# Up-projection of the last 1224 tokens by seven products of halves, in two rounds

## The chip, the cores and the metric

The kernel runs on one core of a Trainium2 chip. The metric is the time of one execution on the device in microseconds (us). The engines are named as in the profile: PE (TensorE, matmuls), PEld (its weight loads), DVE (VectorE), ACT (ScalarE), POOL (GpSimd) and SP (SyncE, which issues the DMAs).

## The reference

One step of a one-layer decoder over 2048 prompt tokens and 8 sample tokens (2056 columns here), width 1024, all in float32. What matters for the change, with h the tokens after attention, pooling and the output projection:

```python
def _mlp(h, g, w_up, w_down):                 # w_up 1024 x 4096, w_down 4096 x 1024
    a = jax.nn.relu(rmsnorm(h, g) @ w_up)
    return (a * a) @ w_down
def _ple(h, p, g, w_gate, w_ple):             # w_gate 1024 x 1024
    gate = jax.nn.sigmoid(rmsnorm(h, g) @ w_gate)
    return (p @ w_ple) * gate
hp = hp + _mixer_out(outs, lses, pooled, w_out[i])
hp = hp + _mlp(hp, norm_mlp_g[i], w_up[i], w_down[i])
hp = hp + _ple(hp, p_prompt[i], ple_norm_g[i], w_ple_gate[i], w_ple[i])
y_prompt = rmsnorm(hp, final_norm_g)
```

The sample tokens go the same way.

## The kernel before, in words

Activations lie transposed: features on the 128 partitions, tokens along the columns. Each float32 operand is split into a high part rounded to fp32r and a low part (the rest), and a product of two operands is three matmuls (high by high, high by low, low by high), so one group over 1024 features is 8 x 3 = 24 matmuls into one PSUM bank (`group`, line 341). `load_w` (line 327) fetches a weight tile by DMA, makes its high part on POOL or ACT and its low part on DVE.

The tokens are taken in two parts: X, the first 832 columns (`CX`, two chunks of 416), and Y, the last 1224 (`CY`, chunks of 416, 416 and 392). After attention the order is: output projection of X, MLP of X, output projection of Y (with the norm of X's gate beside it), gate of X (with the norm of Y's MLP beside it), MLP of Y (lines 1652 to 1670; the final norm and output of X beside its first half), gate of Y's first two chunks, and `last_gate` for the third chunk, with the output of the first two beside it.

`mlp` (line 1319) goes through 4096 hidden features in 8 blocks of 512 for Y. In a block it computes, for each of 4 tiles of 128 hidden features and each chunk, one group of 24 matmuls, then relu, square, the high part (ACT, lines 1344 to 1347) and the low part (DVE); then, for each of 8 output tiles and each chunk, a group of 12 matmuls, which DVE adds to the accumulator held in SBUF (line 1356 on). Weights go through four raw buffers and a ring of two finished tiles.

`Stat` (line 1177) sums squares per token; its `finish` lets PE sum over partitions, DVE and ACT take 1/rms (`newton`), and PE turn the result into a row on all partitions (line 1204). `gate` (line 1397) per output tile: 24 matmuls a chunk, sigmoid (ACT, line 1410), times the embedding part (POOL), added to the accumulator (DVE), square (line 1419), and scaling by the final norm's weight in place (line 1425).

SBUF is cut by hand: `Arena.alloc` gives column ranges of a few large tiles (`mem_f` float32, `mem_r` fp32r, and pieces `ma`, `mb` that change hands between them). A range that is given again waits, instruction by instruction, for the last use of the same columns. Background work (`bg`) is a Python generator that `Pace` advances as groups are written down. The framework orders each engine's instructions ahead of time, by its own cost model, earlier-written work first among what is ready; on the chip each engine runs its list in order.

## Time and profile before

| what | value |
|---|---|
| time, median of 3 runs | 2725.55 us (2722.32 to 2728.67) |
| profiled execution, its own time | 2727.2 us |
| its span, first to last instruction | 2725.4 us |
| instructions | 42893 |
| busy, DVE | 1510.3 us (55%) |
| busy, ACT | 1078.2 us (40%) |
| HBM read / written | 209.47 / 60.30 MB |

Busy time is the time in which an engine has at least one instruction running. Matmuls overlap each other, so the time from one matmul to the next is read from a stretch's length and the count of matmuls in it, not from the duration of one. The span is what the trace covers; the execution's own time is 1.8 us more. In the trace, output projection of Y lies at about 1500 to 1640 us, gate of X to 1735, MLP of Y to 2600, gate of Y to 2717.

### The profile page before, as it was taken

How to read it: one execution, taken by the hardware profiler on the slowest of the kernel's cores; microseconds unless marked ns; L12 is line 12 of the kernel's file. 1: busy time of each engine (PE TensorE's matmuls, PEld its weight loads, DVE VectorE, ACT ScalarE, POOL GpSimd, SP SyncE). 2: the span in 40 equal slices, each digit the busy share in tenths (PEclk: the TensorE clock that was granted, in tenths of full speed). 3: DMA queues.
4: the chain of work that ended last, by engine and by line, in shares of the span. 5: the costliest groups of instructions: out<-in, count | busy, mean ns of one | idle time of the engine just before them, and what ended most of it. 6: DMA issues, size and time to landing. Idle time of an engine off the chain costs nothing.

```text
span 2725.4 us, 42893 instructions
## 1 busy us (share of the span) xinstructions
PE 2645.6 (97%) x15686; PEld 2526.9 (93%) x15686; DVE 1510.3 (55%) x3373; ACT 1078.2 (40%) x2021; POOL 674.8 (25%) x938
## 2 busy tenths in 40 slices
PE   8999899998999999999999899999999999999998
PEld 6888899977988999999999898999999999999998
DVE  6747866665586666665764747432232322322675
ACT  6221354553354355354455424423223123132354
POOL 2414745433253121021222616100000000000163
PEclk9999999999999999999999999999999999999999
DMA  7464344476153333342322545331111111111134
GB/s 249 132 180 121 87 125 125 115 210 191 55 153 107 84 85 86 97 108 71 95 77 66 167 139 152 127 105 39 43 42 40 39 39 39 39 39 39 53 85 150
DMA packets 385936, 272.50 MB, mean 100 GB/s; under 512 B 91466, under 2 KB 349205, under 8 KB 385717
## 3 DMA queue, kind: packets, MB, share of 16 engines
q1 hardware_dynamic: 385653, 269.74, 34.5%
q8 instruction: 123, 2.02, 0.3%
q14 instruction: 88, 0.72, 0.1%
q10 hardware_dynamic: 72, 0.02, 0.0%
HBM read 209.47 MB, written 60.30 MB: 99 GB/s over the span
## 4 chain that ended last, share of the span: by engine, by line
PE 65%; DVE 4%; DMA 4%; POOL 3%; ACT 2%; issue 2%; SPq 0%; DVEq 0%; POOLq 0%; ACTq 0%
PE bank L190 65%; DVE mem_r L196 2%; DVE mem_f L196 1%; POOL mem_ma L196 1%; DMA mem_f<-in_cache_attn_kv_dram 1%; POOL mem_f L196 1%; PE bank L1466 0%; POOL mem_r L199 0%; DMA mem_ma<-poo_s 0%; SPq L187 0%; DVE mem_r L1229 0%; DMA mem_ma<-h_s 0%; DMA mem_f<-poo_s 0%; DVE mem_ma L196 0%; ACT mem_r L931 0%
## 5 line engine op out<-in xcount | busy, mean ns | idle before, releaser
L190 PE MATMUL bank<-mem_r 128*128 128x416 f32 (+10 forms) x13608 | 2447.2, 338 | 42.7 <-DVE mem_f L196 8.1
L190 PEld LDWEIGHTS bank<-mem_r 128*128 128x128 f32 (+2 forms) x13608 | 2305.2, 184 | 118.3 <-DVE mem_f L196 11.9
L196 DVE TENSOR_TENSOR mem_r<-mem_f,mem_r 128x512 fp32r<-128x512 f32 (+3 forms) x568 | 418.2, 742 | 198.9 <-ACT mem_r L335 117.8
L196 DVE TENSOR_TENSOR mem_f<-bank,mem_f 128x416 f32<-128x416 f32 (+3 forms) x488 | 273.4, 567 | 241.4 <-PE bank L190 231.2
L335 ACT CAST mem_r<-mem_f 128x512 fp32r<-128x512 f32 x256 | 157.0, 620 | 575.0 <-PE bank L190 560.5
L196 DVE TENSOR_TENSOR mem_r<-mem_mb,mem_r 128x416 fp32r<-128x416 f32 (+6 forms) x236 | 152.8, 656 | 341.3 <-ACT mem_r L1347 304.1
L199 POOL TENSOR_SCALAR mem_r<-mem_f 128x512 fp32r<-128x512 f32 (+1 forms) x188 | 143.3, 769 | 260.3 <-PE bank L190 177.9
L196 POOL TENSOR_TENSOR mem_ma<-mem_mb,mem_f 128x416 f32<-128x416 f32 x1 | 1.4, 1431 | 828.5 <-ACT mem_f L1205 828.5
L776 DVE CUSTOM_DVE_ANT_0 bank<-bank,mask 128x256 f32<-128x256 f32 (+3 forms) x504 | 159.7, 339 | 40.8 <-PE bank L190 36.6
L1344 ACT ACTIVATE mem_mb<-bank 128x392 f32<-128x392 f32 (+1 forms) x160 | 81.8, 511 | 253.0 <-PE bank L190 253.0
L199 POOL TENSOR_SCALAR mem_r<-mem_r 128x256 fp32r<-128x256 f32 (+1 forms) x117 | 84.1, 731 | 206.3 <-PE bank L190 174.2
L859 POOL TENSOR_SCALAR_AFFINE_SELECT mem_ma<-mem_ma 128x256 f32<-128x256 f32 (+2 forms) x148 | 75.7, 531 | 173.0 <-ACT mem_ma L868 99.2
L196 DVE TENSOR_TENSOR mem_ma<-bank,mem_ma 128x416 f32<-128x416 f32 (+2 forms) x104 | 63.4, 610 | 86.3 <-PE bank L190 76.9
L190 PE MATMUL bank<-mem_mb,mem_r 128*64 128x64 f32 (+4 forms) x494 | 100.6, 323 | 5.7 <-DVE mem_r L196 2.1
L190 PEld LDWEIGHTS bank<-mem_mb,mem_r 128*128 128x128 f32 (+1 forms) x494 | 79.7, 177 | 14.9 <-DVE mem_r L196 2.7
L196 POOL TENSOR_TENSOR mem_f<-mem_f 128x416 f32<-128x416 f32 (+2 forms) x52 | 68.8, 1326 | 96.9 <-DMA mem_f<-in_cache_attn_kv_dram 31.4
L196 DVE TENSOR_TENSOR mem_r<-mem_ma,mem_r 128x512 fp32r<-128x512 f32 (+4 forms) x88 | 63.1, 719 | 39.1 <-ACT mem_r L880 28.3
L859 POOL TENSOR_SCALAR_AFFINE_SELECT mem_mb<-mem_mb 128x256 f32<-128x256 f32 (+2 forms) x76 | 33.7, 463 | 185.1 <-ACT mem_mb L868 126.4
L1345 ACT ACTIVATE mem_mb<-mem_mb 128x416 f32<-128x416 f32 (+1 forms) x128 | 70.0, 547 | 3.8
L199 POOL TENSOR_SCALAR mem_r<-mem_mb 128x512 fp32r<-128x512 f32 (+3 forms) x61 | 51.5, 852 | 77.2 <-PE bank L190 52.4
L1347 ACT CAST mem_r<-mem_mb 128x416 fp32r<-128x416 f32 (+1 forms) x128 | 68.5, 535 | 3.7
L776 DVE DVE_READ_ACCUMULATOR2_ANT mem_ma<- 128x1 f32 (+1 forms) x512 | 68.8, 134 | 0.0
(256 smaller groups left out, 1893.9 us busy)
## 6 DMA issues: line engine op xcount, KB each, us to landing
mem_f<-in_w_up_dram SPq DMA_DIRECT2D x128, 256.0 KB
mem_f<-in_w_down_dram SPq DMA_DIRECT2D x128, 256.0 KB
mem_f<-in_w_in_dram SPq DMA_DIRECT2D x64, 256.0 KB
out_dram<-mem_f SPq DMA_DIRECT2D x55, 256.0 KB
mem_f<-in_cache_attn_kv_dram SPq DMA_DIRECT2D x48, 256.0 KB
mem_f<-in_w_ple_gate_dram SPq DMA_DIRECT2D x48, 256.0 KB
mem_f<-in_x_prompt_dram SPq DMA_DIRECT2D x64, 128.0 KB
xT_s<-mem_f SPq DMA_DIRECT2D x32, 256.0 KB
```

The lines of the kernel that those rows point to most:

```text
L190: PE.matmul(out, l, r, start=start, stop=stop)
L196: eng.tensor_tensor(out, a, b, op=op)
L199: G.tensor_scalar(out, src, 1.0, 1.0, op0=ALU.mult, op1=ALU.mult)
L335: hi(w[:, 0, k0 : k0 + kk], raw)
L776: V.tensor_tensor_reduce(src, src, mask, 1.0, -3e38, ALU.add, ALU.max, mcol[: src.shape[0], col : col + 1])
L859: G.affine_select(out=p, in_=p, pattern=[[0, nblk], [sign, w]], compare_op=ALU.is_ge, fill=0.0, base=base, channel_multiplier=-sign)
L1344: S.activation(a, ps[:, :ln], AF.Relu)
L1345: S.activation(sq, a, AF.Square)
L1347: S.copy(x[:, 0], sq)
```

## The change

Y is cut into four chunks of 306 columns (`HY`). The MLP of Y runs in two rounds (`mlp_seven`), one for each pair of chunks (c0, c1). In a round the up-projection is taken as a product of 2 x 2 blocks: features halved (tile k with tile k + 4), hidden features halved (c with c + 2048), columns halved (c0 with c1). Instead of eight block products there are seven, on sums and differences of the blocks (`w_sums`, `z_sums`, made before the split into high and low parts), each 12 matmuls of 306 columns. PSUM banks 0, 1 and 3 collect them:

```diff
+    SEVEN = ((0, 0, 0, 1), (3, 3, 2, 5), (5, 5, 0, 6), (1, 1, 1, 2), (4, 4, 0, 7), (6, 2, 2, 3), (2, 6, 0, 4))
+    OPENS = (1, 2, 5)
...
+            for slot_w, slot_z, b, p in SEVEN:
+                n, last = 0, 3 * len(x) - 1
+                for k, xk in enumerate(x):
+                    for i, q in PASSES:
+
+                        PE.matmul(bu[b][:, :ln], ws[k // 2].at(slot_w, i, k % 2), xk[:, q, slot_z],
+                                  start=n == 0 and p in OPENS, stop=n == last, skip_group_check=p not in OPENS)
+                        n += 1
+                fill.work(12 * ln)
+                ps = bu[b][:, :ln]
+                if p in (1, 5, 6, 4):
+                    S.copy(z[:, {1: 0, 5: 2, 6: 3, 4: 1}[p]], ps)
+                else:
+                    i = {2: 0, 3: 3, 7: 2}[p]
+                    tt(V, z[:, i], ps, z[:, i], ALU.add)
+                if p == 3:
+                    fill.late()
+            S.activation(z, z, AF.Relu)
+            S.activation(z, z, AF.Square)
+            r = rl[blk, j] = z_parts_view(rls(), 4)
+            S.copy(r[:, 0], z)
+            tt(V, r[:, 1], z, f(r[:, 0]), ALU.subtract)
```

In each tuple stand the weight's slot, the activation's slot, the bank and a number; a product whose number is not in `OPENS` adds to what its bank holds already, after that has been copied out. An up section is seven products and yields 4 x 306 columns of hidden values; a down section is 8 groups of 12 matmuls. `sections` orders them: up 0 (two sections), then up and down sections by turns, up 7 (two sections), then the last four down sections. There are 16 of each in a round.

```diff
+    def w_sums(raw, s):
+        tt(V, s[:, 0], raw[:, 0], raw[:, 3], ALU.subtract)
+        tt(V, raw[:, 3], raw[:, 3], raw[:, 2], ALU.add)
+        tt(V, s[:, 1], raw[:, 3], raw[:, 0], ALU.subtract)
+        tt(V, s[:, 2], raw[:, 1], s[:, 1], ALU.subtract)
...
+        def early(self):
+            w_sums(self.a, self.b)
+            self.p4 = self.parts(self.a, self.w4, 4)
+
+        def late(self):
+            self.p3 = self.parts(self.b, self.w3, 3)
+
+        def parts(self, src, ring, n):
+            w = [x.rearrange("p (s n) -> p s n", s=n) for x in ring()]
+            S.copy(w[0], src)
+            tt(V, w[1], src, f(w[0]), ALU.subtract)
+            return w
```

An up section takes two such weight sets (four tiles of 256 columns read, seven made), a down section two tiles of 1024 columns; both rounds read all of `w_up` and `w_down`. `Fill` loads the next section's weights at a section's start.

`prep_seven` makes a round's activations in four steps: four DMAs from `h1`, two chunks times 1/rms on POOL, ACT and DVE scaling, `z_sums`, and the split of seven slots. For round 1 it runs beside the gate of X; for round 2, beside the last four down sections of round 1. The norm for the gate's first two chunks runs beside the last four down sections of round 2, from a copy of round 1's result in DRAM (`h2`).

The gate of X also writes its result to DRAM (`hxS`), and the final output of X reads it back from there beside the first two up sections of round 1:

```diff
+    bg = prep_seven(h1, rst, g_mlp, xs, CY[:2], zr)
+    gate(xg, lambda ft, ci: hx[ft].ap[:, ci * LC : ci * LC + LC], stx.buf.ap, (0, 1), gate_w(wr), Pace(bg, 4, 24 * NX * 7), dump=hxS)
     drain(bg)
+    for b in (*hx, xg, zr, wr):
+        b.free()
...
+    wp = [R.alloc(n, ("mb",)) for n in (1024, 768, 768, 768)] + [R.alloc(768, ("mc",)), R.alloc(1024, ("r",), low=True)]
+    rlb += [R.alloc(8 * HY, ("r",)) for _ in range(3)]
+    wp += [R.alloc(1024, ("r",)) for _ in range(2)]
+    wa = [b.ap for b in wp]
+    w4 = Turns([(b.ap[:, :1024], b.ap[:, 1024:]) for b in w_ring.b] + [(wa[0], wa[5]), (wa[6], wa[7])])
+    w3 = Turns([wa[1:3], wa[3:5]])
+    zr = Ring.of([F.alloc(7 * HY, ("ma",)), F.alloc(4 * HY, ("ma",))])
+    wf = Ring.of([F.alloc(1024, ("f",), high=True) for _ in range(3)]), Ring.of([F.alloc(768, ("f",), high=True) for _ in range(2)])
...
+    bgx = final_x()
+    fill = Fill(chain(mlp_steps(), mlp_steps()), rings, None)
...
+    def acc_of(src, cols):
+        def get():
+            drain(bgx)
+            acc = [F.alloc(2 * HY) for _ in range(KD)]
+            for ft in range(KD):
+                dma(acc[ft].ap, src[ft * P : ft * P + P, cols])
+            return acc
+        return get
+
+    fill.hook = Pace(bgx, 10, 2 * 7 * 12 * HY * 0.9)
```

`Stat.finish` is split into `begin` (partition sums, 1/rms) and `end` (the turn into rows); in `out_proj` `begin` comes one group and `end` three groups after a chunk's last group, and `end` is kept at that place among PE's instructions; the ends of X's MLP statistics move in the same way into the output projection of Y.

```diff
+            for x in due:
+                x[1] += 1
+                if x[1] == 1:
+                    st.begin(x[0])
+                if x[1] == 3:
+                    st.end(x[0], True)
+            due = [x for x in due if x[1] < 3]
             if ft == KD - 1:
-                done = ci
-        st.finish(done)
+                due.append([ci, 0])
```

The gate of Y becomes three passes over `w_ple_gate` instead of two: chunks 0 and 1 together, chunk 2 with the output of the first two beside it, and `last_gate` for chunk 3 with the output of chunk 2 beside it. The float32 columns of `mem_f` go from 10824 to 9992, with a separate piece `mc` of 832.

## Rows read from the trace of the kernel before

**Rows 1.** The page: its parts 1, 2 and 4.

```profile
PE 2645.6 (97%) x15686; PEld 2526.9 (93%) x15686; DVE 1510.3 (55%) x3373; ACT 1078.2 (40%) x2021; POOL 674.8 (25%) x938
...
GB/s 249 132 180 121 87 125 125 115 210 191 55 153 107 84 85 86 97 108 71 95 77 66 167 139 152 127 105 39 43 42 40 39 39 39 39 39 39 53 85 150
...
PE bank L190 65%; DVE mem_r L196 2%; DVE mem_f L196 1%; POOL mem_ma L196 1%; DMA mem_f<-in_cache_attn_kv_dram 1%; POOL mem_f L196 1%; PE bank L1466 0%; POOL mem_r L199 0%; DMA mem_ma<-poo_s 0%; SPq L187 0%; DVE mem_r L1229 0%; DMA mem_ma<-h_s 0%; DMA mem_f<-poo_s 0%; DVE mem_ma L196 0%; ACT mem_r L931 0%
```

**Rows 2.** Busy time by stretch: length, each engine (instructions), clock, DMA share, GB/s.

```profile
1640.00:1735.00 95.00, 86.43 (x455) 82.82 (x454) 65.80 (x86) 48.27 (x87) 53.27 (x47) 0.98 0.51 147
1930.00:2530.00 600.00, 600.00 (x3240) 595.75 (x3239) 174.86 (x291) 166.06 (x303) 0.00 (x0) 1.00 0.14 41
2600.00:2660.00 60.00, 58.04 (x308) 56.90 (x308) 44.07 (x57) 29.34 (x53) 38.05 (x35) 1.00 0.36 102
2660.00:2725.40 65.40, 55.41 (x346) 52.95 (x345) 35.77 (x61) 27.77 (x48) 21.40 (x24) 0.92 0.48 152
```

**Rows 3.** Groups by shape, TensorE, 1930 to 2530 us: busy us, mean ns.

```profile
L190 PE MATMUL bank<-mem_r 128*128 128x416 f32 x2160 | 415.4, 351 | 0.0
L190 PE MATMUL bank<-mem_r 128*128 128x392 f32 x1080 | 199.7, 340 | 0.0
```

**Rows 4.** Timeline, TensorE: start us, us, instructions.

```profile
645.13 4.96 PE L190 MATMUL bank<-mem_r 128*128 128x264 f32 x39 [0.33 <-DVE mem_r L196]
```

**Rows 5.** Groups by shape, TensorE, 643 to 656 us.

```profile
L190 PE MATMUL bank<-mem_r 128*128 128x264 f32 x48 | 7.4, 292 | 2.8 <-DVE mem_f L1170 2.5 <-DVE mem_r L196 0.3
```

**Rows 6.** Groups by shape, VectorE, 1830 to 2530 us.

```profile
L196 DVE TENSOR_TENSOR mem_r<-mem_f,mem_r 128x512 fp32r<-128x512 f32 x106 | 73.1, 690 | 74.1 <-ACT mem_r L335 74.1
...
L196 DVE TENSOR_TENSOR mem_f<-bank,mem_f 128x392 f32<-128x392 f32 x32 | 18.0, 562 | 20.1 <-PE bank L190 20.1
L196 DVE TENSOR_TENSOR mem_r<-mem_mb,mem_r 128x392 fp32r<-128x392 f32 x27 | 15.3, 567 | 21.4 <-ACT mem_r L1347 21.4
```

**Rows 7.** Groups by shape, ScalarE, 1830 to 2530 us.

```profile
L335 ACT CAST mem_r<-mem_f 128x512 fp32r<-128x512 f32 x106 | 65.8, 620 | 343.5 <-PE bank L190 342.0 <-DMA mem_f<-in_w_down_dram 1.5
...
L1347 ACT CAST mem_r<-mem_mb 128x392 fp32r<-128x392 f32 x27 | 14.0, 520 | 0.8
L1344 ACT ACTIVATE mem_mb<-bank 128x392 f32<-128x392 f32 x27 | 13.3, 493 | 0.0
```

**Rows 8.** Timeline, all engines, where the first gate ends.

```profile
1729.53 0.51 ACT L1410 ACTIVATE mem_ma<-bank 128x416 f32<-128x416 f32 x1
...
1731.32 0.59 DVE L196 TENSOR_TENSOR mem_f<-mem_f,mem_ma 128x416 f32<-128x416 f32 x1 [0.98 <-POOL mem_ma L196]
...
1732.53 0.64 ACT L1425 ACTIVATE mem_f<-mem_f,gcols 128x416 f32<-128x416 f32 x1
...
1733.18 1.03 PE L190 MATMUL bank<-ones,mem_f 128*128 128x1 f32 x8 [0.89 <-DVE mem_f L196]
...
1741.69 0.75 DVE L1474 TENSOR_SCALAR mem_f<-bank,tiny 128x512 f32<-128x512 f32 x1 [2.68 <-PE bank L1466]
```

**Rows 9.** Chain that ended last: start us, us, step.

```profile
1546.21 1.90 DMA h_s<-mem_ma
...
1692.91 3.42 DMA mem_ma<-h_s
```

**Rows 10.** Groups by shape, VectorE, 2600 to 2680 us.

```profile
L196 DVE TENSOR_TENSOR mem_r<-mem_f,mem_r 128x512 fp32r<-128x512 f32 x26 | 24.1, 942 | 2.8 <-POOL mem_r L199 2.8
```

**Rows 11.** Waits of TensorE, 1500 to 1640 us: total, times, longest.

```profile
PE bank L1204 <- DVE tiny L196: 2.4, 2, 1.9
```

**Rows 12.** Waits of TensorE, 1640 to 1735 us.

```profile
PE bank L190 <- ACT mem_ma L1410: 3.2, 3, 1.6
PE bank L190 <- DVE mem_r L196: 2.7, 2, 2.1
PE bank L1204 <- DVE tiny L196: 1.2, 1, 1.2
```

**Rows 13.** Groups by shape, weight loads, whole run.

```profile
L190 PEld LDWEIGHTS bank<-mem_r 128*128 128x128 f32 x12304 | 2185.9, 189 | 95.2 <-DVE mem_f L196 11.9 <-POOL mem_r L199 10.7 <-DVE mem_r L196 5.8
```

More of the change, by code (lines that the diff above doesn't have):

```diff
@@ new lines, in decoder_step, with __init__, early, late @@
+    class Fill:
+        def __init__(self, steps, rings, hook):
+            self.steps, self.rings, self.hook, self.ready, self.open = iter(steps), rings, hook, [], None
+            self.early()
+            self.late()
+        def early(self):
+            step = next(self.steps, None)
+            if step is None:
+                return
+            ws = [kind(self.rings) for kind, _ in step]
+            for w, (_, at) in zip(ws, step):
+                w.load(*at)
+                w.early()
+            self.open = ws
+        def late(self):
+            if self.open is None:
+                return
+            for w in self.open:
+                w.late()
+            self.ready.append(self.open)
+            self.open = None
+        def take(self):
+            ws = self.ready.pop(0)
+            self.early()
+            return ws
+        def work(self, n):
+            if self.hook:
+                self.hook(n)
@@ L1618, in decoder_step, with ends @@
     mp, tp = Turns([bank[0], bank[1], bank[3]]), Turns([bank[2], bank[4], bank[5], bank[6], bank[7]])
-    xg = Acts(CX, keys=("mb", "r"))
-    bg = prep_norm(from_acc(hx, CX), lambda ci: stx.acc[ci], g_ple, xg, (0, 1))
+    xg = Acts(CX, keys=("mb", "r"), high=True)
+    stx.tp = tp
+    def ends():
+        for ci in range(2):
+            stx.end(ci, True)
+        yield
+    bg = chain(ends(), prep_norm(from_acc(hx, CX), lambda ci: stx.acc[ci], g_ple, xg, (0, 1)))
     st = Stat(CY, tp)
-    out_proj(cat, st, h1, wr, Pace(bg, 16, 24 * NY * 7))
+    out_proj(cat, st, h1, wr, Pace(bg, 17, 24 * NY * 7))
     drain(bg)
@@ L1678, in decoder_step @@
+    bg = prep_norm(lambda k, ci, t: where(k, ci), lambda ci: st2.acc[ci - 2], g_ple, xg, (2, 3))
+    gate(xg, where, sums.ap, (0, 1), gate_w(wr), Pace(bg, 16, 24 * 2 * HY * 7))
+    drain(bg)
+    st2.free_acc()
     tp, mp = Turns(bank[2:]), Turns(bank[:2])
```

354 lines of the change are left out of this document (277 added, 77 removed).

## The prediction

> **What bounds the kernel now.** I read the page first. TensorE is busy 97% of the span, VectorE 55%, and the chain that ended last runs through PE for 65% [rows 1]. Busy PE is not yet PE at its peak, so next I read the stretches: from 1930 to 2530 us, inside the MLP of Y, PE is never idle, its clock is 1.00, DVE and ACT are busy under a third of the time and the DMA engines at 0.14 [rows 2]. That stage is bound by the number of matmuls times the time from one to the next. The stretches round it (gate of X, gate of Y) lose time: 86.43 us of PE in 95, 58.04 in 60, 55.41 in 65.4 [rows 2]. So two things decide: what the matmuls cost after the change, and what the edges cost, since a stage without slack cannot win back a wait.
>
> **Matmuls.** From one matmul to the next: 600 us / 3240 = 185.2 ns [rows 2], two thirds of them 416 and one third 392 wide [rows 3], 408 columns in the mean, 0.454 ns a column. No 306 appears. Bounds from the two nearest widths: by 0.454 it takes 138.9 ns. A run of 39 matmuls of 264 columns takes 4.96 us [rows 4]; without the 0.29 us of the last one [rows 5] that is 4.67 / 38 = 122.9 ns, 0.4655 a column, which makes 142.4. The two lie close; I take the middle, 140.65. Counts, before and after: up 32 x 3 x 24 = 2304, then 2 rounds x 16 sections x 7 x 12 = 2688; down 2304, then 2 x 16 x 8 x 12 = 3072; output projection of Y and gate of Y 576 each, then 768 each. Before 5760 x 185.2 = 1066.8 us, after 7296 x 140.65 = 1026.2. **-40.6** (by the bounds -53.4 and -27.8). One eighth of the products goes, and part of it is paid back in shorter matmuls everywhere in Y.
>
> A page weighs against this. The Trainium skill, "TensorE: Matmul & The Clock Gate", section "Back-to-back issue gap", gives about 81 ns a matmul at 128 columns and 131 at 512 in a real stream, so some 64 ns that do not shrink with the columns. By it the sum would be 7296 x 104 against 5760 x 117, 83 us more instead of 40.6 less (an estimate from that page). The trace disagrees: 264 to 408 columns go almost in proportion, 122.9 to 185.2.
>
> **Work beside a section.** At other widths I go by the slopes: DVE (690 - 567) / 120 = 1.025 ns a column from SBUF, ACT (620 - 520) / 120 = 0.833 [rows 6, 7]. DVE then takes 0.43 us at 256, 0.48 at 306 (0.47 out of PSUM), 0.95 at 768, 1.22 at 1024, 1.42 at 1224; ACT 0.42 for 306 out of PSUM, 0.83, 1.05 and 1.21. An up section is 84 x 140.65 = 11.8 us of PE. DVE has three additions out of PSUM 1.42, the low part of the hidden values 1.42, eight weight sums 3.42 and low parts of weights 4.33: 10.6 us. ACT has four copies 1.68, relu, square and high part 3.64, weights 3.76: 9.1. A down section is 13.5 us of PE with 6.2 of DVE and 2.1 of ACT. Where they alternate DVE is busy 16.8 of 25.3 us, and each bank has cover: a product lasts 1.69 us, the copy out of bank 0 takes 0.42, and the last matmul ends 0.15 after the next starts, so 1.1 us is left before the product after next. There I count nothing. Once that cover is gone, PE waits.
>
> **Start of round 1: +12.** `wf` takes its columns from the top of `mem_f`. Following the allocator by hand, the first raw buffer falls on the gate's `pr`, the second on the last two `hx`. So no weight can be fetched before the last tile of X's gate is through: in the trace the last sigmoid starts at 1729.53, the addition ends at 1731.91 (2.4 us later), the scaling in place at 1733.17 (3.6) [rows 8]. Then the second buffer waits for the write to `hxS`, 1.9 us, and is loaded; a 208 KB load took 3.4 [rows 9], and 512 KB at 249 GB/s, the best slice [rows 1], is 1.3 longer: 4.7. Two weight sums and the high part are 0.86 + 1.05. First set at 2.4 + 4.7 + 1.9 = 9.0, second at 3.6 + 1.9 + 4.7 + 1.9 = 12.1, its low part 1.2 later. In before, PE waits 0.9 here [rows 8], since the MLP's weights had been prefetched. SP stands behind these waits too, so the second section's weights follow late. A pause like this also costs clock: 0.92 in the last stretch [rows 2]. Bounds: 5, if X's transposes fill part of it, and 17.
>
> **Up behind up: +7.** Three times a round no down section lies between (0-0, 0-1, 1-0; 7-0, 7-1). The last product's copy from bank 0 then has nothing beside it: 0.6 us each. And ACT has relu, square, high part and two weight parts, 5.7 us, that are written ahead of the first copy of the next section, due after 3.4: up to 2.7 more. I take 1.2 for each of six; bounds 4 and 20.
>
> **First sections of round 1: +3.** X's output adds 7 DVE scalings of 0.75 [rows 8] to two sections: 26.5 us of DVE in 23.6 of PE. The DMAs must bring four weight sets (4.2 MB), X in and out (6.8) and the accumulator (2.5) within 12 + 35 us; at 249 GB/s they need 54. Bounds 0 and 10.
>
> **Between the rounds: +5.** Four down sections are 54 us of PE. DVE: 32 additions 15.2, squares summed 6.7, weights of three sections 7.3, of the next up section 7.8, low part 1.4, `prep_seven` 4 x 5.4 = 21.6: 60 us. Bounds 0 and 10. The end of round 2 has `prep_norm` instead, with less work on DVE: nothing.
>
> **Gate of Y: +3.** With one chunk a tile lasts 3.38 us, in which 512 KB of weights must come, two low parts of 0.94 [rows 10] and two additions of 0.5 lie on DVE, 2.9 in all; a few prefetched tiles help. Bounds 0 and 9. The last tiles' tail stays.
>
> **Ends and gate of X: -6.** PE waits 2.4 and 1.2 us for 1/rms [rows 11, 12]; `end`, three groups later, has it ready: -3.6. In X's gate PE waits 3.2 for the sigmoid's bank and 2.7 for a low part [rows 12], with POOL busy 53 of 95 us [rows 2]; half of the norm's work leaves: I take -2.4. Bounds 0 and -9.5.
>
> **Sum.** -40.6 + 12 + 7 + 3 + 5 + 3 - 6 = -16.6 on the profiled execution's 2727.2, which is span 2725.4 and 1.8 around it: 2710.6. The median lies 1.65 under that execution, so **2709**.
>
> **Rivals.**
> 1. The edges are hidden: X's transposes fill the start, ACT's order puts the copies first. What stays is 5 at the start and 4 at the six seams: -40.6 + 5 + 4 - 6 = -37.6, 2688. For it: DVE and ACT have slack in the sum. Against: the addresses at the start.
> 2. Slower: bank 0 is the neck in every up section. Products 3, 5 and 7 add to a bank that ACT or DVE has just emptied; two long ACT operations ahead of one copy (1.21 + 1.05) pass the 1.1 us by 1.15. 32 x 1.15 = 37, of which 7 are counted: +13, 2739. The gain is gone from (16.6 + 7) / 32 = 0.74 us a section. For it: the order is fixed before the run and DVE is at 90% where up follows up. Against: 66% where they alternate.
> 3. Transfers and seams together, each halfway to its upper bound: 21 us more, 2730. For it: 54 us of DMA in 47. Against: the weights have a section's lead.
> 4. A fixed part: if a third of the 185.2 did not shrink, 306 columns would take 61.7 + 92.6 = 154.3 ns, 7296 x 154.3 = 1125.8, +59 in place of -40.6, with the rest 2808. Against: 264 columns would then take 141.6, and took 122.9 [rows 4]. Nor does the weight load bind: its 189 ns [rows 13] overlap in those same 122.9. The page named above speaks for this one.
>
> **How the numbers follow.** Forecast 0.46 (2699 to 2719 alone), rival 1 0.24, rival 2 0.17, rival 3 0.12, rival 4 0.01. Range 2686 to 2738: it takes in rival 1 and most of rivals 2 and 3. A change under 0.2% (5.5 us) cannot be told from none here. Faster: 0.44 + 0.24 + 0.02 = 0.70. Within 0.2%: 0.02 of the forecast, 0.05 and 0.07 of rivals 3 and 2, 0.14. Slower 0.16.
>
> **What would show it.** 1536 matmuls more. In round 1's alternating part, stretches without PE waits and about 140 ns from matmul to matmul; over 145 and the first term fails. A PE gap of about 10 us after the gate of X, ended by the weights' chain from a DMA into `mem_f`. Waits for bank 0 of about 1 us at the seams, and none elsewhere; if ACT or DVE ends a wait in most up sections, rival 2 is right. DVE near 100% in the last four down sections of round 1. The prediction is wrong if the alternating sections lose time, or if the start of round 1 is filled.

## The result, and the profile after

The changed kernel takes 2760.51 us (median of 4 runs, 2759.41 to 2763.28), the kernel before 2725.82 in the same session: ratio 1.0121, 95% interval 1.011 to 1.0133. It is slower by some 35 us, where 2709 was forecast. One of the four executions of e1_unpin below took 2874.03 us at a granted clock of 0.84, and its ratio and time leave that one out.

The page of the kernel after (span, TensorE's busy time, its granted clock in 40 slices, the chain that ended last), against [rows 1]:

```profile
span 2757.7 us, 47513 instructions
...
PE 2633.6 (96%) x17242; PEld 2511.8 (91%) x17242; DVE 1802.5 (65%) x3918; ACT 1219.7 (44%) x2096; POOL 684.8 (25%) x963
...
PEclk9999999999999999999999899899999899999999
...
PE 60%; DVE 7%; DMA 7%; ACT 3%; issue 2%; POOL 2%; SPq 1%; DVEq 0%; POOLq 0%; ACTq 0%
```

There are 1556 more matmuls and 12 us less of busy PE; the span is 32 us longer. PE's share of the last chain falls from 65% to 60%. So the products are cheaper, and time went where PE does nothing. The windows of after (stretch, its length, busy time and instructions of each engine, granted clock, DMA share, GB/s) show where, against [rows 2]:

```profile
1515.00:1540.00 25.00, 11.37 (x71) 11.03 (x72) 19.40 (x32) 9.99 (x23) 17.70 (x18) 0.71 0.65 174
1660.00:1738.00 78.00, 75.44 (x395) 71.87 (x394) 56.39 (x77) 38.05 (x63) 34.15 (x31) 1.00 0.54 159
1738.00:1758.00 20.00, 9.15 (x41) 8.26 (x40) 9.55 (x24) 8.23 (x13) 3.32 (x4) 0.57 0.69 209
1795.00:2120.00 325.00, 324.84 (x2299) 324.34 (x2298) 195.01 (x331) 141.43 (x171) 0.00 (x0) 1.00 0.28 86
2139.00:2175.00 36.00, 34.89 (x245) 34.42 (x244) 34.83 (x67) 15.66 (x23) 4.58 (x3) 1.00 0.67 197
2175.00:2195.00 20.00, 9.61 (x44) 7.60 (x42) 15.45 (x32) 11.06 (x21) 1.87 (x2) 0.65 0.58 174
2215.00:2530.00 315.00, 314.84 (x2228) 314.34 (x2227) 193.01 (x328) 138.04 (x166) 0.00 (x0) 1.00 0.27 84
2605.00:2757.70 152.70, 133.64 (x928) 128.86 (x926) 105.64 (x178) 72.66 (x144) 78.46 (x88) 0.93 0.46 133
```

The two long stretches are what the change was meant to be: PE never idle, 315 / 2228 = 141.4 ns a matmul, clock 1.00, DVE at 61%. Three short ones have PE busy half of the time and at a clock between its two levels (0.57 to 0.71, where 0.5 is 1.2 GHz and 1.00 is 2.4): the output projection of Y (1515 to 1540), the start of round 1 (1738 to 1758), the end of round 1 (2175 to 2195). The gate of Y and the output behind it (2605 to the end) lose 19 us of 153.

Counted from the first product of each stage to the first of the next, in the trace's list of TensorE's products (us):

| stage | before | after | difference | of it products |
|---|---|---|---|---|
| start of Y's output projection | 1524.4 | 1514.9 | -9.5 | |
| output projection of Y | 115.3 | 144.7 | +29.4 | +1.9 |
| gate of X, to the first up product | 85.1 | 94.6 | +9.6 | 0 |
| MLP of Y | 865.3 | 851.0 | -14.3 | -38.9 |
| gate of Y, output, to the end | 135.3 | 152.4 | +17.1 | +1.9 |

The last column is matmuls by 185.2 and 141.4 ns. So the products save 35 us (5760 x 185.2 less 7296 x 141.4), and the edges lose 77. The -9.5 has no cause of the change that I could find: the projection starts between 1515 and 1525 us in the executions profiled here, and its input tiles shift with it.

### The profile page after: what moved, and what is told of

The parts are those of the page before. It is cut to its first block, busy times and chain, and to the rows that moved or that the text cites. A ratio compares the mean times of both kernels' runs of the same rounds, so it can differ in the third digit from the quotient of the medians.

```text
span 2757.7 us, 47513 instructions
## 1 busy us (share of the span) xinstructions
PE 2633.6 (96%) x17242; PEld 2511.8 (91%) x17242; DVE 1802.5 (65%) x3918; ACT 1219.7 (44%) x2096; POOL 684.8 (25%) x963
## 4 chain that ended last, share of the span: by engine, by line
PE 60%; DVE 7%; DMA 7%; ACT 3%; issue 2%; POOL 2%; SPq 1%; DVEq 0%; POOLq 0%; ACTq 0%
PE bank L193 47%; PE bank L1562 13%; DVE mem_r L199 3%; DVE mem_f L199 2%; DMA mem_ma<-xT_s 1%; DMA h_s<-mem_ma 1%; DVE mem_ma L199 1%; DMA mem_f<-in_cache_attn_kv_dram 1%; SPq L190 1%; DMA mem_ma<-h_s 1%; POOL mem_f L199 1%; DVE mem_r L1246 1%; DMA out_dram<-mem_f 1%; POOL mem_ma L199 0%; DMA mem_f<-poo_s 0%
## 5 line engine op out<-in xcount | busy, mean ns | idle before, releaser
L193 PE MATMUL bank<-mem_r 128*128 128x416 f32 (+10 forms) x11560 | 1987.6, 323 | 47.9 <-DVE mem_r L199 15.0
L193 PEld LDWEIGHTS bank<-mem_r 128*128 128x128 f32 (+2 forms) x11560 | 1800.1, 184 | 120.3 <-DVE mem_r L199 23.3
L199 DVE TENSOR_TENSOR mem_r<-mem_f,mem_r 128x512 fp32r<-128x512 f32 (+6 forms) x550 | 449.2, 826 | 168.1 <-ACT mem_r L1470 40.6
L199 DVE TENSOR_TENSOR mem_f<-bank,mem_f 128x306 f32<-128x306 f32 (+4 forms) x590 | 304.9, 522 | 143.5 <-PE bank L193 136.6
L1562 PE MATMUL bank<-mem_r 128*128 128x306 f32 x1472 | 233.1, 306 | 8.7 <-ACT mem_r L1440 4.6
L1562 PEld LDWEIGHTS bank<-mem_r 128*128 128x128 f32 x1472 | 215.7, 190 | 11.1 <-ACT mem_r L1440 5.1
L193 PE MATMUL bank<-mem_r,mem_mb 128*128 128x306 f32 (+2 forms) x928 | 202.0, 303 | 2.1 <-DVE mem_mc L782 1.6
L199 DVE TENSOR_TENSOR mem_f<-mem_f 128x256 f32<-128x256 f32 (+4 forms) x321 | 150.1, 483 | 74.8 <-DMA mem_f<-in_w_up_dram 52.6
L1562 PE MATMUL bank<-mem_r,mem_mb 128*128 128x306 f32 x1024 | 180.1, 306 | 1.1 <-ACT mem_ma L1568 0.7
L199 DVE TENSOR_TENSOR mem_r<-mem_ma,mem_r 128x512 fp32r<-128x512 f32 (+3 forms) x146 | 144.9, 998 | 31.0 <-ACT mem_r L886 16.5
L1562 PEld LDWEIGHTS bank<-mem_r,mem_mb 128*128 128x128 f32 x1024 | 155.7, 190 | 2.9 <-ACT mem_ma L1568 2.6
L193 PEld LDWEIGHTS bank<-mem_r,mem_mb 128*128 128x128 f32 x928 | 154.2, 189 | 3.0 <-DVE mem_mc L782 1.9
L1470 ACT CAST mem_r<-mem_f 128x1024 fp32r<-128x1024 f32 x60 | 60.5, 1046 | 106.4 <-PE bank L1562 93.9
```

The source lines that it names most:

```text
L193: PE.matmul(out, l, r, start=start, stop=stop)
L199: eng.tensor_tensor(out, a, b, op=op)
L1470: S.copy(w[0], src)
L1562: PE.matmul(bu[b][:, :ln], ws[k // 2].at(slot_w, i, k % 2), xk[:, q, slot_z], start=n == 0 and p in OPENS, stop=n == last, skip_group_chec ...
```

## The experiments

Every edit stands against the kernel after, if nothing else is said; ratios are to the kernel before, run beside it, with 95% intervals. "Loss" of a stretch is its length less its products at their steady distance (141 ns at 306 columns, 190 at 416): waits and lower clock together. It shifts by a few us with the price put on the short transposes and sums in a stretch, so it serves to compare runs. It is 29 us in 1500 to 1600, 27 in 1700 to 1800, 21.5 in 2100 to 2300, 31.5 from 2500 on; in before 14, 6, 0 and 14.

### First round: one suspect each

**e1_unpin**, `stx.end(ci, True)` becomes `stx.end(ci)`.

> One edit on the changed kernel: the turning of X's 1/rms into rows is no longer kept at its written place among TensorE's instructions. Theory: in the changed kernel TensorE stands 10.5 and 3.1 us before the partition sums of X (1525 and 1537 us), because the kept instruction bars later output-projection matmuls from being put in front of it; freed, the planner fills the wait as it did in the kernel before (two waits of 1.9 and 0.5 us there). Expected 12 to 18 us less than 2760.5: about 2746, and the stretch 1510 to 1640 us 12 us shorter. Rival: VectorE and GpSimd finish the squares of X too late whatever stands in front, and the matmuls of Y wait for their own inputs; then the time stays within 3 us of 2760.5.

2763.52 (three executions), 1.0125 (1.0104 to 1.0146). No time is gained; the order pin isn't the cause.

**e2_wf_low**

```
-  wf = ... F.alloc(1024, ("f",), high=True) ... F.alloc(768, ("f",), high=True)
+  wf = ... F.alloc(1024, ("f",), low=True) ... F.alloc(768, ("f",), low=True)
```

> One edit on the changed kernel: the raw weight buffers of the MLP of Y are taken from the low end of the float32 memory, over the gate's own weight buffers and the first output tiles of X, which are done some 9 us or more before the gate of X ends, instead of over its last output tiles. Theory: the pause at 1738 to 1754 us (6.1, 2.0, 2.0 and 0.8 us without a matmul, clock 0.57) is the wait of the first weights for that memory; with it gone the first up section starts 8 to 14 us earlier: about 2750. Rival: the pause is the gate's own elementwise tail (three sigmoids 3.4 us apart after the last matmul), which holds ScalarE and VectorE so that weights in memory would be split no earlier; then under 3 us are gained, 2758 or more.

2759.48, 1.012 (1.0095 to 1.0144). The first up product starts 11 us sooner, and then stops twice. PE's timeline in this run (start, length, what runs, in brackets the idle time ahead and what ended it):

```profile
1743.55 1.25 PE L1562 MATMUL bank<-mem_r 128*128 128x306 f32 x6
1747.89 1.90 PE L1562 MATMUL bank<-mem_r 128*128 128x306 f32 x6 [3.09 <-ACT mem_ma L1669]
1753.21 3.43 PE L1562 MATMUL bank<-mem_r 128*128 128x306 f32 x12 [3.42 <-ACT mem_r L1470]
```

Once the sigmoid (L1669) of X's gate still holds a bank, once the high part (L1470) of the second weight set is late. The address of the raw buffers held back the first product, and nothing behind it.

**e3_zsums_pool**, `z_sums(z, G)` in round 2's preparation; **e4_keep_w**, the gate's weights kept between the passes in Y's gate.

> One edit on the changed kernel: the sixteen activation sums of round 2 (four a step, made beside the last four down sections of round 1) run on GpSimd, which is idle there, instead of VectorE. Theory: VectorE is full from about 2120 us on (60 us of work beside 54 us of products), and the first products of round 2 wait for the activations it finishes last (waits of 1.3 to 4.3 us between 2176 and 2192 us, 21 us lost in all with the low clock); with 7.7 us taken off VectorE, 6 to 12 us come back: about 2751. Rival: the chain of four steps through one buffer (DMA, GpSimd, ScalarE, VectorE) sets the end, not the sum of VectorE's work; GpSimd's additions, about 1 us each against 0.47, make a step 2 us longer and the time grows by 3 to 8 us: 2764 to 2768.

2763.19, 1.0127 (1.0108 to 1.0145); loss between the rounds 19.3 for 21.5.

> One edit on the changed kernel: the gate's weights for chunk 3 are not fetched and split again; the eight finished tiles of chunk 2's pass are kept (two more tile buffers). Theory: the third pass over the weights loads DMA, GpSimd and VectorE (8 x 2 low parts and high parts), and with them gone the gate of Y loses 4 to 8 us less: about 2754. Rival: the losses there (2.4 us at 2634, 2.2 at 2667, 3.2 at 2686 us, with the low clock behind each) come at the change of pass and from the 1/rms of the output of chunks 0 and 1, in the second pass, where the weights are still fetched; then 2 us or less is gained.

2762.41, 1.0126 (1.0108 to 1.0143); loss in Y's gate 28.8 for 31.5. Neither gain is seen in the time. Each is read from one execution: between the rounds, runs that leave the stretch alone scatter by some 3 us, and k3_best, which has e3's edit, shows no gain there, so only e4's is likely to be real.

### Second round: the rival behind each

**f1_xsq_dve**, `Stat(CX, tp, G)` becomes `Stat(CX, tp)`.

> The squares of X's output are summed on VectorE instead of GpSimd; nothing else is changed. In the trace of after PE waits 3.13 and 10.50 us at 1522 and 1526 us in front of the products of these sums with ones, then runs about 17 us at a lower clock. Theory A (GpSimd is the neck): it does 16 such additions of 1.1 to 1.3 us in order between Y's tiles of the output projection's input, which wait for their own transfers; without them the sums are ready some 10 us sooner and Y's tiles too. Expected: the two waits together under 4 us, 10 to 17 us less in all, about 2747. Rival B (the place of the products with ones): they stand 48 matmuls after the start of the projection; VectorE, 14.0 of 15 us busy between 1510 and 1525, becomes the neck in GpSimd's place (16 x 0.6 = 10 us more of it), the wait is ended by VectorE and stays over 8 us, time within 4 us of 2760.

2764.42, 1.0126 (1.0105 to 1.0148). In after PE stops in front of X's sums of squares, and GpSimd has the last of them at 1536.77. PE and GpSimd of after:

```profile
1514.95 7.03 PE L193 MATMUL bank<-mem_r 128*128 128x306 f32 x48 [1.10 <-DVE mem_f L199]
1525.11 1.23 PE L193 MATMUL bank<-ones,mem_f 128*104 128x1 f32 x8 [3.13 <-POOL mem_f L199]
1536.83 1.54 PE L193 MATMUL bank<-ones,mem_f 128*104 128x1 f32 x8 [10.50 <-POOL mem_f L199]
```

```profile
1535.71 1.06 POOL L199 TENSOR_TENSOR mem_f<-mem_f 128x416 f32<-128x416 f32 x1
1536.74 0.84 POOL L202 TENSOR_SCALAR mem_r<-mem_f 128x512 fp32r<-128x512 f32 x1
```

With the sums on DVE the two waits are 2.19 and 4.21 instead of 3.13 and 10.50, but DVE is full (15.00 of 15 us in the window 1515 to 1530 of this run). The projection takes 140 us for 145; it starts at 1525, the late end of the range above, which can't be put down to the edit, and no time is gained:

```profile
1515.00:1530.00 15.00, 13.51 (x71) 12.62 (x70) 15.00 (x27) 6.51 (x16) 7.86 (x8) 0.89 0.63 171
```

**f2_late_begin**

```
 def ends():
+    for _ in range(6): yield
+    for ci in range(2): stx.begin(ci, True)     # was at the end of mlp()
+    yield; yield
     for ci in range(2): stx.end(ci, True)
```

> The first half of X's 1/rms (products of the sums with ones, and the Newton steps) is written six background steps into Y's output projection instead of ahead of it, and held there; GpSimd still sums the squares. Theory B (the place): PE has about 190 matmuls of the projection, 27 us, in front of the products with ones instead of 48, 7 us; the waits of 3.13 and 10.50 us go, and with them most of the time at the lower clock: 12 to 20 us less, about 2744. Rival A (GpSimd is the neck): Y's tiles come out of the same list of GpSimd, the last at about 1535 us, so PE waits for mem_r of those tiles instead, together over 8 us, and the time moves by less than 5 us.

2764.65, 1.0135 (1.012 to 1.015). The waits for X's sums are gone, and one longer one stands in the same place:

```profile
1539.06 21.12 PE L193 MATMUL bank<-mem_r 128*128 128x306 f32 x134 [16.62 <-POOL mem_r L202]
```

It waits for the fourth piece of `w_out`, cast by GpSimd at 1538; SyncE had issued its load behind Y's input tiles, at 1532 in after, where before has it issued by 1515. SyncE of after, then of before:

```profile
1532.35 0.43 SPq L190 DMA_DIRECT2D mem_f<-in_w_out_dram  x1
```

```profile
1513.79 1.51 SPq L187 DMA_DIRECT2D mem_f<-in_w_out_dram  x2
```

**f3_gate_prep**, on e2: `Pace(bg, 4, 24 * NX * 7)` of X's gate becomes `24 * NX * 4`.

> On top of e2_wf_low (raw weight buffers at the low end of mem_f, 2759.5) the four preparation steps of round 1 are spread over the first half of X's gate (4 of 8 tiles' work) instead of seven eighths of it. Theory C: ScalarE's list holds the preparation's scalings and casts between the gate's sigmoids, so that the last tiles come 5.2 to 5.5 us apart instead of 4.5 and ScalarE ends the gate three banks (some 10 us) behind PE; with the preparation done early it catches up, and the first product of round 1 starts 5 to 9 us sooner: about 2751, time lost by PE between 1700 and 1800 us 24 down to about 16. Rival D: the gate's own chain (sigmoid, product, addition, square) is what sets the end, and the preparation only moves the wait into the middle of the gate: PE waits there instead, gain below 3 us.

2761.72, 1.0121 (1.0106 to 1.0136). Loss 23 for 24 in e2; PE now waits inside the gate (2.19, 0.96, 0.58 us for the sigmoid's bank) and still 3.08 and 4.19 behind it. That is rival D.

**f4_no_loads**, in `prep_seven` of round 2 the loads of k = 1, 2, 3 are left out.

> Leaves out the loads of h1 in the last three of the four preparation steps of round 2 (12 transfers of 128x306; these steps work on what the buffer holds, so the last 612 tokens are not computed rightly). VectorE's work stays what it is. Theory E (one buffer in a chain): in after GpSimd waits 14.6, 16.2 and 11.9 us for these transfers, since they cannot start before the step ahead has given back the one z buffer, so that a step takes 13 to 18 us and the last ends 10 us after the last product of round 1; without the transfers a step is 3 us shorter, the last ends about 9 us sooner, and of the 21 us lost between 2150 and 2210 about 10 go: 2750. Rival F (VectorE is full): it is busy 34.8 of 36 us between 2139 and 2175, and its amount of work sets the end of the preparation; loss and time stay within 4 us.

2761.86, 1.0122 (1.0107 to 1.0138). GpSimd's scalings, one at the head of each preparation step (after, then this run):

```profile
2139.70 1.40 POOL L199 TENSOR_TENSOR mem_ma<-mem_ma 128x612 f32<-128x612 f32 x1 [386.26 <-DMA mem_ma<-rst_s]
2155.67 2.29 POOL L199 TENSOR_TENSOR mem_ma<-mem_ma 128x612 f32<-128x612 f32 x1 [14.57 <-DMA h_s<-mem_f]
2174.11 1.39 POOL L199 TENSOR_TENSOR mem_ma<-mem_ma 128x612 f32<-128x612 f32 x1 [16.15 <-DMA mem_ma<-h_s]
2187.44 1.37 POOL L199 TENSOR_TENSOR mem_ma<-mem_ma 128x612 f32<-128x612 f32 x1 [11.94 <-DMA mem_ma<-h_s]
```

```profile
2157.50 1.39 POOL L199 TENSOR_TENSOR mem_ma<-mem_ma 128x612 f32<-128x612 f32 x1 [12.11 <-DVE mem_r L199]
2175.06 1.50 POOL L199 TENSOR_TENSOR mem_ma<-mem_ma 128x612 f32<-128x612 f32 x1 [16.18 <-DVE mem_r L199]
2186.97 1.48 POOL L199 TENSOR_TENSOR mem_ma<-mem_ma 128x612 f32<-128x612 f32 x1 [10.41 <-DVE mem_r L199]
```

The steps stay 12 to 18 us apart without their loads; what ends the wait is now DVE. That is rival F: DVE's list, where a step's operations (two scalings, four sums, two low parts) stand between the additions and weight sums of four sections.

### Third round: mending the edges

**g1_wout_early**, on f2: the first four loads of `w_out` are written behind the last `dw` of X's MLP.

> On top of f2_late_begin: the first four loads of w_out are written behind the last weight load of X's MLP instead of behind all of Y's input tiles. In f2_late_begin PE stood 16.6 us until 1539 for the low or high part of the fourth of these pieces; in after its load was issued by SyncE at 1532.35, behind some 28 transfers of Y's input tiles, in before the fourth piece was issued at 1513.8. Theory G (place in SyncE's list): with the piece loaded at about 1500 its cast is done by about 1515, PE runs on through the second and third chunk; the 16.6 us and most of the 17 us at the lower clock go: 14 to 20 us less than f2, about 2748. Rival H (GpSimd's list is long whatever the order): the cast, or Y's last input tiles, still come out of GpSimd at 1535 or later, PE waits over 8 us for them, gain under 5 us.

2760.36, 1.012 (1.0103 to 1.0137). The load goes out at 1507; PE runs 25 products more and then waits for DVE, which waits for the residual `xT`, issued at 1538.78, again behind Y's input tiles:

```profile
1542.65 19.71 PE L193 MATMUL bank<-mem_r 128*128 128x306 f32 x120 [10.63 <-DVE mem_ma L199]
```

```profile
1538.78 1.00 SPq L190 DMA_DIRECT2D mem_ma<-xT_s  x2
```

**g2_gate_pipe**, on e2: in `gate` the sigmoid of a tile is written ahead of the product, addition, square and scaling of the tile before.

> On top of e2_wf_low: in the gates of X and Y (all but the last pass) the sigmoid of a tile is written ahead of the product, addition, square and scaling of the tile before, so that ScalarE doesn't stand between a sigmoid and its own square. Theory I (the gate's chain through ScalarE's list): in after a tile's sigmoid starts 3.4 us after the one before even with nothing else to do, 5.2 to 5.5 with preparation between, and ScalarE ends X's gate 10 us behind PE; with the sigmoids first the banks come free at once, the first product of round 1 starts 5 to 9 us sooner, and passes 1 and 2 of Y's gate lose 2 to 5 us less: 2747 to 2752. Rival J (filling the first weights): VectorE's 16 sums and 8 low parts and ScalarE's casts for the first two sets, some 13 us of VectorE that can only start when the loads are in, set the first product; the gate's end moves, the first product doesn't: gain below 4 us.

2762.32, 1.0124 (1.0101 to 1.0146); loss 23.3 for 24.3. The first up product starts at 1745.25, and PE waits 3.07 us for a sigmoid and 3.42 for the second weights' high part, as in e2. The gain is under 4 us as rival J has it, though the product that is late is not the first.

**g3_relief**, from `last_1` to the end of round 1 `Stat(CY[:2], tpx, G, nsq=1)` and `w_sums` on GpSimd.

> From the last four down sections of round 1 on, GpSimd instead of VectorE adds the squares (14 additions) and makes the weight sums of the next up section (8); the rest is as in after. Takes some 10 of VectorE's 52 us between 2139 and 2195. Theory F (VectorE is full and the preparation stands in its list): the four preparation steps take 3 us less each, their last part is done about 8 us sooner, and of the 21.5 us lost between 2100 and 2300 about 8 to 12 go: 2750. Rival E (the chain through one buffer sets it: load, GpSimd, ScalarE, VectorE, ScalarE, VectorE one after the other): the steps stay at 12 us or more, gain below 4 us. Rival K: GpSimd's additions hold up its own scaling of the next step, and the steps become longer: slower than after by up to 5 us.

2767.23, 1.0144 (1.0129 to 1.0159): slower by some 6 us, at the edge of what the intervals tell, and the loss between the rounds is 5 us more than in after; rival K. Eight weight sums hold GpSimd for 8.4 us (1.05 each, where DVE takes 0.42), and the last scaling of the preparation starts at 2196.85 instead of 2187.44:

```profile
2145.44 8.38 POOL L199 TENSOR_TENSOR mem_f<-mem_f 128x256 f32<-128x256 f32 x8 [0.95 <-DMA mem_f<-in_w_up_dram]
...
2196.85 1.37 POOL L199 TENSOR_TENSOR mem_ma<-mem_ma 128x612 f32<-128x612 f32 x1 [4.24 <-DMA mem_ma<-h_s]
```

Nor did DVE come free, so this run can't tell theory F from rival E: it is busy 34.32 of 36 us from 2139 (34.83 in after), with 49 instructions for 67. The preparation's sixteen sums, still on DVE, take longer. By shape on DVE, 2100 to 2215 us (count, busy us, mean ns), in after, then in this run, and the stretch in this run:

```profile
L199 DVE TENSOR_TENSOR mem_ma<-mem_ma 128x306 f32<-128x306 f32 x16 | 7.6, 473 | 2.0 <-ACT mem_ma L1514 2.0
```

```profile
L199 DVE TENSOR_TENSOR mem_ma<-mem_ma 128x306 f32<-128x306 f32 x16 | 11.1, 696 | 6.2 <-ACT mem_ma L1517 6.0
```

```profile
2139.00:2175.00 36.00, 33.58 (x231) 32.43 (x229) 34.32 (x49) 15.00 (x23) 18.67 (x16) 1.00 0.56 169
```

Eight of the sixteen overlap a GpSimd instruction and take 0.92 us in the mean; the other eight take 0.47.

**g4_all**, g1 + g2 + g3.

> The edits of g1_wout_early, g2_gate_pipe and g3_relief together. If theories G, I and F hold and the losses are separate, the gains add: 17 + 8 + 9 = 34 less than 2761, about 2727, no slower than before. If the rivals hold, or if a wait that goes at one edge is made good at the next, it stays above 2750.

2763.8, 1.0134 (1.0119 to 1.0149). Nothing adds up. Each mended wait was followed by the next in another engine's list, within a few us of the old end.

### Fourth round: what the edges carry

**j1_no_prep**

```
 for k in range(KD // 2):                       # prep_seven, both rounds
+    if k: xs.append(xs[0]); yield; continue
-bg = prep_norm(... g_ple, xg, (2, 3))           # gate of Y
+xg.b[k, ci + 2] = xg.b[k, ci]
```

> Leaves work out: of the four preparation steps of each round only the first is done (its result stands in for the other three), and in Y's gate chunks 2 and 3 read the input of chunks 0 and 1, so that their preparation falls away; the outputs of the last 1224 tokens are not the right ones. All matmuls, weights and edges stay. Theory M (preparation is the price of the edges): what is left out is 3 x 5.4 us of VectorE, 12 loads and their places in SyncE's, ScalarE's and GpSimd's lists in X's gate, the same between the rounds, and 16 tiles in Y's gate; then the loss between 1700 and 1800 us falls from 27 to under 15, between 2100 and 2300 from 21.5 to under 5, between 2500 and 2758 from 31.5 to under 22, in all about 38 us less: 2722. Rival N (filling the weights, the additions and 1/rms set the ends): the losses fall by under 4, 6 and 3 us: above 2748.

2727.12, 0.9986 (0.9973 to 0.9999): 37 us less than after by the ratios. Loss 16.9 for 27.2 at the start of round 1, 4.1 for 21.5 between the rounds, 21.1 for 31.5 in Y's gate. Theory M holds here. The windows of this run over the start of round 1 and the end of round 1, where PE now runs at the full clock:

```profile
1741.00:1761.00 20.00, 14.11 (x79) 12.79 (x78) 12.78 (x28) 9.81 (x14) 1.16 (x2) 0.74 0.88 269
...
2120.00:2180.00 60.00, 59.14 (x423) 58.92 (x423) 45.20 (x90) 25.98 (x40) 1.40 (x1) 1.00 0.56 167
2180.00:2200.00 20.00, 19.17 (x138) 18.91 (x137) 13.82 (x28) 12.58 (x18) 0.00 (x0) 1.00 0.33 101
```

**j2_rden**, on g1: the rows of 1/denominator come for two chunks in one load, 16 loads for 32.

> On top of g1_wout_early: the rows of 1/denominator for Y's input tiles are loaded for two chunks at a time, 16 loads in place of 32 in SyncE's list (all work is done). In g1 PE stood 10.6 us in front of the second group of the output projection until VectorE could add the residual, whose load stands in SyncE's list behind the tiles' loads (SyncE needs 0.33 to 0.57 us for each). Theory O (SyncE's list is the neck of this stage): 16 x 0.5 = 8 us sooner, the wait falls to under 4 us and most of the 13.7 us at the lower clock go; the loss between 1500 and 1600 falls from 29.7 to under 17, the time to about 2747. Rival P (GpSimd, ScalarE and VectorE make a tile in 1.7 us whatever SyncE does): the last tile is still done at 1535 or later, gain under 4 us.

2759.62, 1.01 (1.0081 to 1.012). The wait falls to 7.53 us (theory O asked for under 4), the loss in 1500 to 1700 from 41.7 (g1) to 31.8; some 6 us less than after by the ratios, no more than the intervals can tell. Between O and P: SyncE's list is part of it; the tiles still come 1.64 us apart.

**j3_idle**, 70 transposes behind X's gate and 60 ahead of round 2 that nobody reads.

> The kernel after with transposes that nobody reads on TensorE where it waits: 70 of 128x128 behind the last product of X's gate, 60 ahead of round 2. Theory Q (a large part of an edge is the clock that PE loses by waiting): with PE busy the granted clock in 1738 to 1758 stays near 1.00 instead of 0.57, and in 2175 to 2195 near 1.00 instead of 0.65, and the work behind runs at full speed: 5 to 8 us less at each of the two edges, 2748. Rival R (the other engines set the end): the clock stays up, but PE stands again in front of the next weights or preparation, gain below 3 us; if the transposes (130 x 0.15 us = 20 us) stand in the way of products that are ready, up to 8 us slower.

2771.61, 1.0149 (1.0134 to 1.0164): 8 us slower. The clock is 1.00 while they run, and falls right behind them, since PE then waits 4.82 us for a load of `hxS`. The 60 came to lie behind the waits of round 1's end, so that edge wasn't tested.

```profile
1738.00:1748.00 10.00, 10.00 (x83) 9.92 (x82) 4.38 (x7) 5.52 (x10) 2.83 (x3) 1.00 0.41 126
1748.00:1768.00 20.00, 11.71 (x71) 10.90 (x69) 11.59 (x27) 8.29 (x12) 0.70 (x2) 0.74 0.69 203
```

**k1_no_prep_cat**, j1 and, for Y's input tiles of the output projection, `xa.b[k, ci] = Shared(xa.b[k, ci - 2])` for chunks 2 and 3; **k2_before_no_prep**, the kernel before with chunk 0 standing in for chunks 1 and 2 in the input tiles and the MLP's input, and for chunk 2 in the gate's.

> Leaves out what j1_no_prep leaves out, and also Y's input tiles of the output projection for chunks 2 and 3 (chunks 0 and 1 stand in for them), 16 of 32 tiles with their loads; the outputs of the last 1224 tokens are not the right ones. Theory M (preparation is the price of the edges): the loss between 1500 and 1600 us falls from 29.7 to 14 or less, the others stay as in j1_no_prep (2727): about 2711, 16 below before; that leaves of the change what its matmuls save. Rival T (the first edge hangs on w_out, the residual loads and X's sums, which stay): it falls by under 5 us, above 2722.

2707.22, 0.9905 (0.989 to 0.9919). The loss in 1500 to 1600 is 10.3 for 29.7.

> The control: the kernel before, with the same kind of work left out. Y's input tiles for chunks 1 and 2 (16 of 24), the MLP's input of chunks 1 and 2 (16 of 24) and the gate's input of chunk 2 (8) are not made, chunk 0 stands in; the outputs of the last 1224 tokens are not the right ones. Theory M with the cover: before hides this work beside its longer products, so leaving it out gives under 12 us of its 49 us of loss behind 1400 us: 2715 to 2725. Rival U (preparation costs as much in either kernel): 25 us or more less, under 2702, and then the change would have inherited the price of its edges, not made it.

2707.74, 0.9905 (0.9888 to 0.9921). My theory that before hides this work falls: it pays some 26 us for it, the changed kernel 1.0121 - 0.9905, 59 us (the spans of the profiled executions give 19 and 52, the same difference). So the change inherited a part of the price and more than doubled it. The windows of k1 (output projection, last product of X's gate to first of round 1, start of round 1, Y's gate), and of k2:

```profile
1521.00:1644.00 123.00, 116.94 (x813) 115.66 (x812) 64.19 (x127) 31.08 (x63) 37.41 (x37) 0.97 0.39 111
1719.00:1729.00 10.00, 5.39 (x27) 4.81 (x26) 4.65 (x15) 5.34 (x8) 1.16 (x2) 0.66 0.85 259
1729.00:1780.00 51.00, 47.75 (x323) 45.39 (x322) 37.48 (x63) 27.92 (x38) 0.00 (x0) 0.97 0.77 236
...
2564.00:2705.60 141.60, 128.34 (x927) 125.69 (x925) 87.52 (x158) 66.31 (x128) 63.77 (x76) 0.96 0.49 144
```

```profile
1521.00:1632.00 111.00, 110.87 (x620) 109.56 (x619) 60.98 (x105) 28.70 (x52) 36.76 (x36) 1.00 0.44 131
1632.00:1708.00 76.00, 74.92 (x404) 73.55 (x403) 41.38 (x62) 36.34 (x63) 35.36 (x34) 1.00 0.42 126
1708.00:1760.00 52.00, 52.00 (x303) 51.37 (x302) 14.60 (x28) 23.96 (x44) 1.28 (x2) 1.00 0.31 106
2572.00:2706.00 134.00, 123.15 (x710) 119.01 (x709) 73.34 (x120) 60.55 (x104) 56.26 (x57) 0.97 0.40 120
```

Without the preparation before runs from the output projection into the MLP with PE idle for 1.2 us in 239. The changed kernel loses 6 us in the projection, 4.6 and 3.3 at the start of round 1, and has a longer gate of Y. By stages as in the table above, k1 against k2: +12.4, +7.8, -28.0, +7.9: zero. The two leave out not quite the same (40 of 72 tiles in k2; 32 of 64 tiles and 6 of 8 steps of four tiles in k1; 16064 and 17136 columns). With the products taken off as there, +10.5, +7.8, +10.9 and +6.0 are left: of the 77 us that the edges lose against before, 35 stay, as much as the products save. Whether these hang on the preparation that k1 still does or on something else, no run here tells.

**k3_best**, j2 with e2, g2 and e3, with all work done.

> All work done: j2_rden with the gates' sigmoids first and the weights low (g2_gate_pipe) and the sums of round 2's preparation on GpSimd (e3_zsums_pool). If the gains seen in the stretches add up (10 us before 1700, 4 at the start of round 1, 2 to 3 between the rounds, 2 in Y's gate): 2745. By theory M none of them takes preparation away, each wait is followed by the next: 2752 to 2762.

2759.85, 1.0093 (1.0067 to 1.012). It is the best ratio with all work done; its interval overlaps that of after, its four executions lie between 2751.38 and 2765.81, and it doesn't reach the kernel before.

## Why the prediction was wrong, point by point

The span came out 32 us longer where the sum had it 16.6 shorter. Of these 49 us the ends of X account for 31, the seam between the rounds for 16.5, the gate of Y for 12 and the products for 5; the start of round 1 with the gate of X for nothing, the seams and first sections for -7, and the earlier start of the projection for -9.5.

- **Matmuls, -40.6.** Right in kind, a little large: 141.4 ns instead of 140.65, -35.2. Rival 4 is out: a third part that doesn't shrink asked for 154.3. The Trainium skill's "TensorE: Matmul & The Clock Gate", section "Back-to-back issue gap", by which the estimate was 104 ns, does not agree with this trace's 141.4.
- **Alternating sections, nothing.** Right: 324.84 of 325 us and 314.84 of 315 of PE, with DVE at 60 and 61% (66 forecast). Rival 2, bank 0 as the neck, isn't there; its time of 2739 was passed for another reason.
- **Up behind up, +7.** Smaller: the trace of after has waits of 0.60 and 0.35 us at 1782 and 1783 and of 0.90 and 0.40 at 2205 and 2211, 2 to 3 us. With them the first sections of round 1 (+3, two more waits of 0.65 and 0.51) and these seams come to some 3 us of the 10 forecast.
- **Gate of X and start of round 1, -2.4 and +12.** Together as forecast, +9.6 in the table, but by luck: the gate gives 6.4 and the gap costs 16.0. The lines there, against [rows 8] (PE, then the last sigmoid on ACT and the first weight sum on DVE):

```profile
1736.82 1.49 PE L193 MATMUL bank<-mem_r 128*128 128x416 f32 x7
1744.41 1.44 PE L193 MATMUL bank<-ones,mem_f 128*128 128x1 f32 x6 [6.10 <-DVE mem_f L199]
1747.84 1.74 PE L193 MATMUL bank<-ones,mem_f 128*128 128x1 f32 x8 [1.99 <-DVE mem_f L199]
1751.53 1.94 PE L1730 MATMUL bank<-ident,mem_f 128*128 128x128 f32 x8 [1.96 <-DMA mem_f<-hx_s]
1754.27 1.90 PE L1562 MATMUL bank<-mem_r 128*128 128x306 f32 x6 [0.80 <-ACT mem_r L1470]
...
1744.31 0.50 ACT L1669 ACTIVATE mem_ma<-bank 128x416 f32<-128x416 f32 x1
...
1751.89 0.42 DVE L199 TENSOR_TENSOR mem_f<-mem_f 128x256 f32<-128x256 f32 x1 [2.05 <-DMA mem_f<-in_w_up_dram]
```

  The chain that I followed came nearly as forecast: from the last sigmoid to the first weight sum 7.6 us (7.1 in the sum), to the first product 10.0 (9.0). I counted it from that sigmoid and left out that PE's last product of the gate ends 6.0 us before it, at 1738.31. And the buffers' addresses were not the only thing in the way: e2 took those away and g2 the gate's order, and the first product came 9 to 11 us sooner, but the second set's high part and the sigmoids held up the next ones until 1753 and 1756. j1 shows that 10 of the 27 us hang on the preparation beside them.
- **Ends of X, -3.6: the step that failed first.** I took the 2.4 and 1.2 us of [rows 11, 12] away and asked nothing about what else lies in the output projection of Y. It came out 27.5 us worse, products aside. I never costed the input tiles: 32 for 24, each with its loads in SyncE's list and its place in GpSimd's, ACT's and DVE's. ACT casts one every 1.76 us in after (2.07 in before), and the last one at 1536.3, 21 us behind the projection's first product, where before has it at 1534.9, 10.5 behind: 11 us later. X's sums, the last piece of `w_out` and the residual all stand behind them in some list; f1, f2 and g1 met them one after the other. k1 leaves half of the tiles out, and 19 of the 29 us of loss are gone.
- **Between the rounds, +5: mis-sized.** I summed DVE (60 us beside 54 of PE) and took the difference. The sum agrees with the trace: DVE is busy 34.83 of 36 us until 2175. But the preparation is a chain of load, GpSimd, ACT, DVE, ACT and DVE through one buffer, in lists that are full; its steps take 13 to 18 us where 5.4 of DVE were counted, so its last part is done at 2196, 19 us after the last product of round 1. j1, with three of the four steps left out: 4.1 left of 21.5. f4 shows that the loads are not what sets the steps; the chain's other links weren't taken apart.
- **Gate of Y, +3: mis-sized.** +15 products aside. e4: the weights are 2 or 3 of it, if that gain is real. j1: 10 is the preparation of chunks 2 and 3. The rest (2 us at a change of pass, 3 at a sigmoid behind the output's 1/rms) wasn't taken apart.
- **What all of them share.** The change makes shorter chunks. They give the same number of preparing operations, or more, and less PE time to lie beside, and the three edges that failed were each counted as a sum on one engine, or not at all. PE's granted clock also fell where it waited: 0.57, 0.65 and 0.71 in the three short windows. The sum counted that nowhere but in the bounds of one edge.
- **Rivals.** None at its place. The time lies 22 us above the slowest one that was given a real chance (2739), since the three mis-sized edges were thought of one at a time.

## What to carry to other kernels

Cutting a long stage's products into more and shorter ones makes the stage cheaper and its neighbours dearer: before counting the gain, list what must be prepared in the stretch ahead of it and follow one item through every engine's list, as a chain and not as a sum on the busiest engine. When mending one wait moves nothing, leave a whole class of work out, in the kernel before as well: that tells the price in a run or two, where eleven single edits told only which list the wait had moved to. What is left between the two kernels then (35 us here) is the part that is still to be explained.
